# Norm scale and bias taken out of the transitions of a two-layer trunk, and low parts of weights moved to VectorE

## The chip, the cores and the metric

The kernel runs on one core of one Trainium2 chip. TensorE does the matmuls, VectorE, ScalarE and GpSimd the elementwise work, and SyncE (SP in the profile) issues most of the transfers between device memory (HBM) and the core's memory (SBUF); a few are issued by GpSimd. The metric is the time of one execution on the device, in microseconds. The kernel before has a median of 1731.97 us over three runs (1730.14 to 1737.19).

## The reference

One step of a trunk of two layers (`DEPTH` = 2) on 128 context tokens and 512 latent tokens: 640 rows of 1024 numbers, in five tiles of 128 rows (tile 4 holds the context tokens, and comes last in the order of work). Layer 0 mixes tokens by differential attention, layer 1 by neighbourhood attention; each is followed by an MLP with a squared ReLU, 1024 to 4096 and back. Every sub-layer has this form, for latent and context tokens with their own modulation:

```python
h = x * (1 + scale) + shift                                  # scale, shift, gate: SiLU(cond) @ w_mod + b_mod
x = layer_norm(ALPHA * x + gate * sublayer(h), ln_g[i, s], ln_b[i, s])

def layer_norm(x, g, b):
    mu = jnp.mean(xf, -1, keepdims=True)
    var = jnp.mean(jnp.square(xf - mu), -1, keepdims=True)
    return (xf - mu) * lax.rsqrt(var + LN_EPS) * g + b

def sq_relu_mlp(h, w1, w2):
    return jnp.square(jax.nn.relu(h @ w1)) @ w2
```

So there are four norms: after layer 0's attention, after its MLP, after layer 1's attention, and after its MLP (the output). Three of them lie at a transition into a further sub-layer.

## The kernel before

**Precision and weights.** Each operand of a matmul is held as a high part (rounded, `hi`) and a low part (what is left, `lo`), and each product is three matmuls (`mm3`, L119 to L121: high by high, low by high and high by low). Weights come in pieces of 128 x 2 x 512 numbers. `pump` (L175) issues the load of the next piece into one of three buffers `raw` on SyncE; `conv` (L190) has ScalarE cast it to `wh` (L194) and then makes the low part `wl` = raw - `wh` in two halves of 128x512 (L196). `self.pool_lo` says which engine takes a half: with 0 both go to VectorE, with 1 the odd half to GpSimd, with 2 both to GpSimd. A ring of five converted pieces is kept: when the last matmul of a piece is placed, `done` converts the piece that comes five later and issues a further load.

**Order.** TensorE's order is written by hand: `ORDER0`, `ORDER1` and `ORDER_LN` are lists of names, and `run` calls the function that `op` put under each name. What the other engines do is ordered by a scheduler, which sets each instruction into its engine's queue; a queue is worked off in order. So an instruction that waits holds up what stands behind it in its queue.

**Transitions.** X holds the 640 rows in SBUF. In layer 0 and layer 1 the output projection is done in two column halves per tile (o and j in the order lists). `gated` (g) multiplies the product in PSUM by the gate (L1161, into `tmp`), adds it to X (L1163, L1165), takes statistics (L1028), and `ln_pre` makes the mean and variance (L1034), the square root on ScalarE, the reciprocal (L1037), and one pass of 128x1024 over the tile (L1038): (x - mean) * rstd, in place. `norm` (h) calls `ln_h`: TensorE transposes the tile in eight pieces (L1067), ScalarE applies per-row scale and bias while it copies out of PSUM, and the result is split into `hhi` and `hlo` (L127). The norm's own scale g and bias b are at this place folded into the modulation (`mod_affine`), because TensorE needs only h; X itself, which the next residual sum needs, gets them by `affine` in `ln_h`: two passes of 128x1024 per tile on GpSimd (L1078 and L1079). After attention the names of `lnt` hold g and b, the passes of all five tiles are called by the last name of the order list, W (`close`), and the scheduler puts them where they fit. f0 to f3 are the first columns of the MLP's first up chunk.

**MLP (`rest`).** Four groups `gr`; in each, two up chunks of 512 columns (c = 0, 1; `ff`, with `act` for the activation: a Relu on ScalarE, L1224, a product on VectorE, L1225, and a split) and then a down product in two column halves, added to X with the gate (`add_gated_sb`, L1111 to L1117). During attention `pool_lo` is 1, from the swap into the output projection on 2, and in the MLP 1. After the last group of layer 0, `ORDER_LN` runs per tile the second down half (n: `down`), the norm (h: `ln_h`) and the first products of layer 1 (v); here `affine` follows directly and its result goes to device memory (`x1`) for the residual of layer 1.

Of the kernel before, what the change touches and what calls it, by code (L numbers as in the profile page):

```python
# [49 lines left out]
    g1 j02 j13 h0 g2 j03 j04 h1 j14 g3 g4 h2 f0 f2 h3 f3 h4 f1 W  # L50
# [10 lines left out]
    h4 f3 f2 W  # L61
# [4 lines left out]
class Net:  # L66
# [604 lines left out]
    def layer0_attn(self, acc0):  # L671
        nc, a = self.nc, self.a
        with self.tc.tile_pool(name="at0", bufs=1) as pool:
            self.q0 = pool.tile([P, 4, NT], F32R, name="q0")
            self.Vs, self.QKs = {}, {}
            self.pool_lo = 1
# [90 lines left out]
            first4 = self.proj_ops(pool, 0, late, EARLY0, "S73", ("N6", "N7"), ("E0", 2, "E1"), ln)  # L767
# [177 lines left out]
    def layer1_attn(self, pre):  # L945
        nc, a = self.nc, self.a
        with self.tc.tile_pool(name="at1", bufs=1) as pool:
            self.pool_lo = 1
# [24 lines left out]
            def early():  # L973
                self.pool_lo = 2
# [12 lines left out]

            def ln():
                ts = [pool.tile([P, D], F32, tag="PT", name=self.nm("lnt"), bufs=3) for _ in range(2)]
                for t, n in zip(ts, ("lng", "lnb")):  # L990
                    nc.gpsimd.dma_start(t, a[n][1, 0].partition_broadcast(P))
                return ts
# [27 lines left out]
            first4 = self.proj_ops(pool, 1, late, EARLY1, "S73", ("Y", "Z"), ("E", 6, "E"), ln)  # L1020
# [38 lines left out]
    def ln_h(self, pool, X, t, g, b, AB, dst, tag=("hs", 2), now=True):  # L1059
# [57 lines left out]
    def proj_ops(self, pool, l, late, early, free, ready, tag, ln):  # L1117
        nc, n, op = self.nc, NCH * l + 6, self.op
        seq = [(hf, t) for hf in range(2) for t in range(NTT)]
        accs, ms, sb, fs, first, tail = {}, {}, [], [], {}, []  # L1120
# [85 lines left out]
    def rest(self, l, X, first):  # L1206
# [3 lines left out]
        with self.tc.tile_pool(name=f"mlp{l}", bufs=1) as pool:  # L1210
# [9 lines left out]
            def act(us, k, src, cs=None):  # L1220
# [3 lines left out]
                nc.scalar.activation(rv, src, AF.Relu)  # L1224
                nc.vector.scalar_tensor_tensor(rv, src, 0.0, rv, ALU.max, ALU.mult)  # L1225
                self.split(us[0][:, k, cs], us[1][:, k, cs], r[:, cs])
                if not quiet:
                    next(mods, None)

            for gr in range(4):  # L1230
                us = [pool.tile([P, KT, NT], F32R, tag=t, name=self.nm(t)) for t in ("uhi", "ulo")]
                for c in range(2):
                    n = C0 + 8 + 4 * gr + c
                    if gr == 0 and c == 0:
# [9 lines left out]
                        g, b = self.ln_tiles(pool, l, 1)  # L1244
                        st = self.sml.tile([P, NTT, 2, 6], F32, tag="st", name=self.nm("st"), bufs=2)
                        continue
                    for fp in range(2):
                        quiet = gr == 0
                        fs = (2 * fp, 2 * fp + 1)
                        for f in fs:  # L1250
# [12 lines left out]
            def down(t, n):  # L1263
# [150 lines left out]
```

## Time and profile before

| what | value |
|---|---|
| median of three runs | 1731.97 us (1730.14 to 1737.19) |
| profiled execution, its span | 1732.1 us (the page gives no other time of it) |
| TensorE busy | 1645.9 us, 95% |
| VectorE busy | 1131.4 us, 65% |
| ScalarE busy | 662.1 us, 38% |
| GpSimd busy | 594.5 us, 34% |

Busy time is time in which an instruction of the engine was running. The engines work side by side, so these shares don't add up to the span; what an instruction off TensorE costs is seen only where TensorE waits. The trace names the engine, the line, the tiles written and read, and for an idle time the instruction that ended it. The granted clock is a share of TensorE's full clock of 2.4 GHz; 0.50 is its lower level, 1.2 GHz.

### The profile page before, as it was taken

How to read it: one execution, taken by the hardware profiler on the slowest of the kernel's cores; microseconds unless marked ns; L12 is line 12 of the kernel's file. 1: busy time of each engine (PE TensorE's matmuls, PEld its weight loads, DVE VectorE, ACT ScalarE, POOL GpSimd, SP SyncE). 2: the span in 40 equal slices, each digit the busy share in tenths (PEclk: the TensorE clock that was granted, in tenths of full speed). 3: DMA queues.
4: the chain of work that ended last, by engine and by line, in shares of the span. 5: the costliest groups of instructions: out<-in, count | busy, mean ns of one | idle time of the engine just before them, and what ended most of it. 6: DMA issues, size and time to landing. Idle time of an engine off the chain costs nothing.

```text
span 1732.1 us, 25928 instructions
## 1 busy us (share of the span) xinstructions
PE 1645.9 (95%) x10026; PEld 1455.4 (84%) x10026; DVE 1131.4 (65%) x2015; ACT 662.1 (38%) x1338; POOL 594.5 (34%) x457
## 2 busy tenths in 40 slices
PE   8999999999699999999998999998889999999997
PEld 5788888777698988989887889997779898898996
DVE  4788778765848789798557577868685343242338
ACT  2456545643531322221324565655353132131321
POOL 2111012113722337154247243342383133424322
PEclk9999999989899999999999999999989999999999
DMA  8432334233144445454223222223123131212221
GB/s 328 147 118 84 100 113 148 80 112 108 57 133 151 159 146 172 142 164 144 77 83 118 89 78 79 77 85 133 61 92 106 59 98 50 97 56 91 81 66 61
DMA packets 59086, 187.96 MB, mean 109 GB/s; under 512 B 7396, under 2 KB 14034, under 8 KB 57938
## 3 DMA queue, kind: packets, MB, share of 16 engines
q1 hardware_dynamic: 55890, 174.89, 31.3%
q0 software_dynamic: 3072, 11.40, 1.8%
q8 instruction: 79, 1.29, 0.3%
q14 instruction: 45, 0.37, 0.1%
HBM read 176.25 MB, written 7.40 MB: 106 GB/s over the span
## 4 chain that ended last, share of the span: by engine, by line
PE 75%; DVE 14%; issue 4%; POOL 4%; ACT 3%; DMA 1%; SPq 0%; DVEq 0%; POOLq 0%; ACTq 0%
PE M L119 14%; PE M L121 14%; PE M L120 14%; PE S L121 8%; PE S L119 7%; PE S L120 7%; DVE wl L196 4%; PE S L452 2%; PE S L454 2%; POOL wl L196 2%; DVE hlo L127 1%; PE M L589 1%; PE M L259 1%; DVE X L1038 1%; POOL X L1078 1%
## 5 line engine op out<-in xcount | busy, mean ns | idle before, releaser
L196 POOL TENSOR_TENSOR wl<-rw,wh 128x512 fp32r<-128x512 f32 x209 | 345.3, 1672 | 591.4 <-ACT wh L194 541.0
L194 ACT CAST wh<-rw 128x1024 fp32r<-128x1024 f32 x192 | 196.9, 1050 | 348.3 <-PE M L121 268.5
L121 PE MATMUL S<-hhi,wl 128*128 128x320 f32 (+1 forms) x944 | 293.4, 311 | 6.1 <-DVE wl L196 4.7
L119 PE MATMUL S<-hhi,wh 128*128 128x320 f32 (+1 forms) x944 | 292.7, 310 | 0.0
L120 PE MATMUL S<-hlo,wh 128*128 128x320 f32 (+1 forms) x944 | 291.9, 309 | 0.0
L119 PE MATMUL M<-wh,uhi 128*128 128x512 f32 x640 | 249.6, 390 | 1.0 <-ACT uhi L126 1.0
L121 PE MATMUL M<-wh,ulo 128*128 128x512 f32 x640 | 249.3, 389 | 0.3
L120 PE MATMUL M<-wl,uhi 128*128 128x512 f32 x640 | 249.2, 389 | 0.0
L196 DVE TENSOR_TENSOR wl<-rw,wh 128x512 fp32r<-128x512 f32 x175 | 208.9, 1213 | 52.3 <-ACT wh L194 51.3
L119 PE MATMUL M<-wh,hhi 128*128 128x256 f32 (+1 forms) x640 | 202.4, 316 | 9.3 <-DVE tmp L1161 8.4
L121 PE MATMUL M<-wh,hlo 128*128 128x256 f32 (+1 forms) x640 | 196.4, 307 | 3.8 <-DVE hlo L127 3.8
L120 PE MATMUL M<-wl,hhi 128*128 128x256 f32 (+1 forms) x640 | 196.2, 307 | 1.8 <-DVE wl L196 1.8
L121 PEld LDWEIGHTS S<-hhi,wl 128*128 128x128 f32 x944 | 178.9, 189 | 10.1 <-DVE wl L196 8.3
L119 PEld LDWEIGHTS S<-hhi,wh 128*128 128x128 f32 x944 | 179.3, 190 | 0.2
L120 PEld LDWEIGHTS S<-hlo,wh 128*128 128x128 f32 x944 | 179.1, 190 | 0.2
L293 DVE SCALAR_TENSOR_TENSOR jk<-wm,cb 128x1024 bf16<-128x1024 f32 x96 | 142.5, 1484 | 1.5
L121 PEld LDWEIGHTS M<-wh,ulo 128*128 128x128 f32 x640 | 120.2, 188 | 26.3 <-DVE ulo L127 1.1
L119 PEld LDWEIGHTS M<-wh,uhi 128*128 128x128 f32 x640 | 120.2, 188 | 26.2 <-ACT uhi L126 1.9
L120 PEld LDWEIGHTS M<-wl,uhi 128*128 128x128 f32 x640 | 120.1, 188 | 24.6
L119 PEld LDWEIGHTS M<-wh,hhi 128*128 128x128 f32 x640 | 124.2, 194 | 18.6 <-DVE tmp L1161 8.9
L1225 DVE SCALAR_TENSOR_TENSOR r<-S,r 128x640 f32<-128x640 f32 (+1 forms) x62 | 48.4, 781 | 137.8 <-ACT r L1224 137.7
L121 PEld LDWEIGHTS M<-wh,hlo 128*128 128x128 f32 x640 | 123.8, 193 | 11.7 <-DVE hlo L127 7.0
(280 smaller groups left out, 3026.6 us busy)
## 6 DMA issues: line engine op xcount, KB each, us to landing
rw<-in_w SPq DMA_DIRECT2D x192, 512.0 KB, 4.2
wm<-in_wmodT SPq DMA_DIRECT2D x48, 512.0 KB, 3.6
rw<-in_wmod SPq DMA_DIRECT2D x32, 512.0 KB, 4.5
wm<-in_wmod SPq DMA_DIRECT2D x8, 1024.0 KB, 10.5
gate<-gates POOLq DMA_DIRECT2D x6, 512.0 KB, 5.0
X<-in_xT SPq DMA_DIRECT2D x8, 320.0 KB, 11.1
X<-in_xn SPq DMA_DIRECT2D x5, 512.0 KB, 5.4
x<-X SPq DMA_DIRECT2D x5, 512.0 KB, 2.8
```

The lines of the kernel that those rows point to most:

```text
L119: te.matmul(out, sh, mh, start=start, stop=False)
L120: te.matmul(out, sh, ml, start=False, stop=False)
L121: te.matmul(out, sl, mh, start=False, stop=stop)
L127: nc.vector.tensor_tensor(lo, src, hi, ALU.subtract)
L194: keep(nc.scalar.copy(hi, r))
L196: keep(eng.tensor_tensor(lo[:, k], r[:, k], hi[:, k], ALU.subtract))
L259: self.nc.tensor.matmul(acc[32 * j : 32 * j + 32, :256], self.sc[:, 4 * r + j, :], w[:, j, :], start=r == 0, stop=r == 1, tile_position=(0 ...
L293: op = nc.vector.scalar_tensor_tensor(jk, ws[t], 1.0, cb[:, x, :], ALU.mult, ALU.mult, accum_out=mc[:, t, x : x + 1])
L452: te.matmul(out[x], Q[:, x, q], k(K[:, x]), start=True, stop=False)
L454: te.matmul(out[x], Q[r, lo[x], q], k(K[r, x]), start=False, stop=True)
L589: nc.tensor.transpose(t[:, P * (j - j0) : P * (j - j0) + P], E[:, P * j : P * j + P], self.idf)
L1225: nc.vector.scalar_tensor_tensor(rv, src, 0.0, rv, ALU.max, ALU.mult)
```

## The change

1. `pool_lo` is 0 in both attentions, in their output projections too, and 0 from the last down product of an MLP on. In the MLPs it is still 1, and at the program's start still 2. Of 209 low halves on GpSimd 87 move to VectorE.
2. After attention, `close` and the name W are gone, and so are the tiles `lnt`. The ten passes over X (`affine`) are called in the MLP instead, after the Relu of the first column group of the second up chunk in group 0, and the first pass of each tile gets a dependency on that Relu. The tiles `lng` and `lnb` of the MLP are first loaded with this norm's g and b, and loaded anew behind the passes with those of the MLP's norm.
3. At the end of layer 0's MLP, `ln_mid` takes the place of `ln_pre` and the two passes on GpSimd: two passes of 128x1024 on VectorE, (x - mean) * g and x * rstd + b, and the store of the tile directly behind. `mod_affine` for layer 1's attention is then 1 + scale and shift alone.

```diff
@@ ORDER0, and ORDER1 alike
-    g1 j02 j13 h0 g2 j03 j04 h1 j14 g3 g4 h2 f0 f2 h3 f3 h4 f1 W
+    g1 j02 j13 h0 g2 j03 j04 h1 j14 g3 g4 h2 f0 f2 h3 f3 h4 f1
@@ mod_affine
-        pl, ps = (l, 0) if s == 1 else (l - 1, 1)
-        g = self.lnc[:, pl, ps, 0, :].unsqueeze(2).to_broadcast([P, KT, 2])
-        b = self.lnc[:, pl, ps, 1, :].unsqueeze(2).to_broadcast([P, KT, 2])
+        g = self.lnc[:, l, 0, 0, :].unsqueeze(2).to_broadcast([P, KT, 2])
+        b = self.lnc[:, l, 0, 1, :].unsqueeze(2).to_broadcast([P, KT, 2])
+        if s == 0:
+            nc.vector.tensor_scalar(AB[:, 0], sc, 1.0, None, ALU.add)
+            nc.vector.tensor_copy(AB[:, 1], sh)
+            return
@@ layer0_attn, and layer1_attn alike
-            self.pool_lo = 1
+            self.pool_lo = 0
             def swap():
-                self.pool_lo = 2
-            def ln():
-                t = pool.tile([P, 2, D], F32, tag="aTh", name="lnt")
-                for x, n in enumerate(("lng", "lnb")):
-                    nc.gpsimd.dma_start(t[:, x, :], a[n][0, 0].partition_broadcast(P))
-                return t[:, 0, :], t[:, 1, :]
@@ behind ln_pre
+    def ln_mid(self, st, X, t, g, b, dst):
+        nc, x, sml = self.nc, X[:, t, :], self.sml
...
+        nc.vector.bn_aggr(mv, st[:, t, :, :])
+        nc.scalar.activation(rs, mv[:, 1:2], AF.Sqrt, bias=self.eps)
+        nc.vector.scalar_tensor_tensor(x, x, mv[:, 0:1], g, ALU.subtract, ALU.mult)
+        nc.vector.reciprocal(rs, rs)
+        nc.vector.scalar_tensor_tensor(x, x, rs, b, ALU.mult, ALU.add)
+        nc.sync.dma_start(dst, x)
+
+    def affine(self, X, t, g, b, after):
+        nc, x = self.nc, X[:, t, :]
+        op = nc.gpsimd.tensor_tensor(x, x, g, ALU.mult)
+        self.tc.add_manual_dep(
+            op.ins, after.ins.name,
+            mybir.DependencyInfo(mybir.DependencyClass.Sync, mybir.DependencyReason.DATA), reason="affine",
+        )
+        nc.gpsimd.tensor_tensor(x, x, b, ALU.add)
@@ ln_h
-        def affine():
-            nc.gpsimd.tensor_tensor(x, x, g, ALU.mult)
-            nc.gpsimd.tensor_tensor(x, x, b, ALU.add)
-            if dst is not None:
-                nc.sync.dma_start(dst, x)
-
-        if now:
-            affine()
-        return affine
@@ rest
-                        g, b = self.ln_tiles(pool, l, 1)
+                        g, b = self.ln_tiles(pool, l, 0)
...
-                            act(us, 4 * c + f, s2[:, :, :320])
+                            op = act(us, 4 * c + f, s2[:, :, :320])
+                            if gr == 0 and f == 0:
+                                for t in range(NTT):
+                                    self.affine(X, t, g, b, op)
+                                g, b = self.ln_tiles(pool, l, 1)
...
-                    self.ln_pre(st, X, t)
+                    self.ln_mid(st, X, t, g, b, self.x1[t])
...
+            self.pool_lo = 0
             for t in range(NTT):
                 down(t, 0)
```

What this does to the queues is seen at three places. In the rows below x2 is two instructions in a row, `X_4337` the residual, `wl`, `wh` and `rw` a weight's low part, high part and raw piece, `st`, `mv` and `rstd` the norm's statistics. Since lines were taken out and added, L1078/L1079 of before answer to L1042/L1047 of after, L1038 to L1027 (and in the MLP's norm to L1035/L1037), L1028 to L1017, L1034 to L1023 or L1033, L1161 to L1159, L1111/L1115 to L1110/L1114.

GpSimd's queue at the end of the first transition and on into the first MLP, before:

```order
L1078 TENSOR_TENSOR X_4337<-X_4337,lnt 128x1024
L1079 TENSOR_TENSOR X_4337<-X_4337,lnt 128x1024
L1078 TENSOR_TENSOR X_4337<-X_4337,lnt 128x1024
L1079 TENSOR_TENSOR X_4337<-X_4337,lnt 128x1024
L1078 TENSOR_TENSOR X_4337<-X_4337,lnt 128x1024
L1079 TENSOR_TENSOR X_4337<-X_4337,lnt 128x1024
L1214 DMA cb<-srow 128x1024 x2
L1089 DMA gate_932_5430<-gates 128x1024
L1089 DMA gate_933_5432<-gates 128x1024
L1089 DMA lng_5434<-in_lng 128x1024
L1089 DMA lnb_5436<-in_lnb 128x1024
L196 TENSOR_TENSOR wl_5380<-rw_4862,wh_5379 128x512
```

The same place after:

```order
L196 TENSOR_TENSOR wl_5367<-rw_4862,wh_5366 128x512
L196 TENSOR_TENSOR wl_5380<-rw_5002,wh_5379 128x512
L196 TENSOR_TENSOR wl_5393<-rw_5039,wh_5392 128x512
L196 TENSOR_TENSOR wl_5406<-rw_5371,wh_5405 128x512
L1042 TENSOR_TENSOR X_4337<-X_4337,lng_5421 128x1024 x2
L1047 TENSOR_TENSOR X_4337<-X_4337,lnb_5423 128x1024 x2
L1042 TENSOR_TENSOR X_4337<-X_4337,lng_5421 128x1024 x2
L1047 TENSOR_TENSOR X_4337<-X_4337,lnb_5423 128x1024 x2
L1042 TENSOR_TENSOR X_4337<-X_4337,lng_5421 128x1024
L1047 TENSOR_TENSOR X_4337<-X_4337,lnb_5423 128x1024
L1088 DMA lng_5490<-in_lng 128x1024
L1088 DMA lnb_5492<-in_lnb 128x1024
```

Before, the passes stand ahead of the MLP's loads of gates and norm rows, and the MLP's low halves come behind; after, four odd low halves of the MLP come first, then all ten passes together, then two loads, and the next low halves behind these.

VectorE's queue in the first transition, from the statistics of tile 2 to those of tile 3 (`tmp` the gated product), before:

```order
L1034 BN_AGGR mv_4981<-st_4898 128x2
L1163 TENSOR_TENSOR X_4337<-X_4337,tmp_5044 128x512
L1161 TENSOR_TENSOR tmp_5048<-S_4782,gate_4321 128x512
L1037 RECIPROCAL rstd_4983<-rstd_4983 128x1
L127 TENSOR_TENSOR hlo<-hs_5008,hhi 128x4x128
L1038 TENSOR_SCALAR X_4337<-X_4337,mv_4981,rstd_4983 128x1024
L1028 BN_STATS st_4898<-X_4337 128x6
L1165 SCALAR_TENSOR_TENSOR X_4337<-X_4337,tmp_5048 128x512
L127 TENSOR_TENSOR hlo<-hs_5020,hhi 128x4x128
```

The same place after:

```order
L1023 BN_AGGR mv_4978<-st_4898 128x2
L196 TENSOR_TENSOR wl_4998<-rw_4836,wh_4997 128x512 x2
L1026 RECIPROCAL rstd_4980<-rstd_4980 128x1
L127 TENSOR_TENSOR hlo<-hs_5005,hhi 128x4x128
L1027 TENSOR_SCALAR X_4337<-X_4337,mv_4978,rstd_4980 128x1024
L1161 TENSOR_TENSOR X_4337<-X_4337,tmp_5041 128x512
L1159 TENSOR_TENSOR tmp_5045<-S_4782,gate_4321 128x512
L127 TENSOR_TENSOR hlo<-hs_5017,hhi 128x4x128
L196 TENSOR_TENSOR wl_5035<-rw_4849,wh_5034 128x512 x2
L1017 BN_STATS st_4898<-X_4337 128x6
```

Four low halves, which stood in GpSimd's queue, are now between the norm's steps, two ahead of the reciprocal of tile 2 and two ahead of the next statistics.

VectorE's queue in the second transition, tiles 0 and 1 of the norm behind the first MLP (`lng`, `lnb` the norm's rows), before:

```order
L1028 BN_STATS st_5438<-X_4337 128x6
L1034 BN_AGGR mv_8670<-st_5438 128x2
L1037 RECIPROCAL rstd_8672<-rstd_8672 128x1
L1038 TENSOR_SCALAR X_4337<-X_4337,mv_8670,rstd_8672 128x1024
L1111 TENSOR_TENSOR tmp_8701<-M_8676,gate_932_5430 128x512
L1115 TENSOR_TENSOR X_4337<-X_4337,tmp_8701 128x512
L1028 BN_STATS st_5438<-X_4337 128x6
L1034 BN_AGGR mv_8705<-st_5438 128x2
L127 TENSOR_TENSOR hlo<-hs_8712,hhi 128x4x128
L1037 RECIPROCAL rstd_8707<-rstd_8707 128x1
L1038 TENSOR_SCALAR X_4337<-X_4337,mv_8705,rstd_8707 128x1024
```

The same place after:

```order
L1017 BN_STATS st_5425<-X_4337 128x6
L1033 BN_AGGR mv_8668<-st_5425 128x2
L1035 SCALAR_TENSOR_TENSOR X_4337<-X_4337,mv_8668,lng_5490 128x1024
L1036 RECIPROCAL rstd_8669<-rstd_8669 128x1
L1037 SCALAR_TENSOR_TENSOR X_4337<-X_4337,rstd_8669,lnb_5492 128x1024
L1110 TENSOR_TENSOR tmp_8701<-M_8676,gate_932_5417 128x512
L1114 TENSOR_TENSOR X_4337<-X_4337,tmp_8701 128x512
L1017 BN_STATS st_5425<-X_4337 128x6
L1033 BN_AGGR mv_8705<-st_5425 128x2
L1035 SCALAR_TENSOR_TENSOR X_4337<-X_4337,mv_8705,lng_5490 128x1024
L1036 RECIPROCAL rstd_8706<-rstd_8706 128x1
L127 TENSOR_TENSOR hlo<-hs_8714,hhi 128x4x128
```

One pass over the tile behind the reciprocal has become two, the first of which stands ahead of the reciprocal.

## Rows read from the trace of the kernel before

**Rows 1.** the page: span, and busy time of each engine

```profile
span 1732.1 us, 25928 instructions
...
PE 1645.9 (95%) x10026; PEld 1455.4 (84%) x10026; DVE 1131.4 (65%) x2015; ACT 662.1 (38%) x1338; POOL 594.5 (34%) x457
```

**Rows 2.** busy time by stretch: start and end, length, engines, granted clock, DMA

```profile
415.00:475.00 60.00, 44.88 (x243) 38.72 (x242) 52.28 (x66) 29.14 (x69) 44.48 (x26) 0.89 0.19 60
890.00:945.00 55.00, 48.16 (x273) 42.06 (x273) 45.11 (x51) 27.56 (x64) 38.81 (x25) 0.94 0.38 126
1230.00:1302.00 72.00, 59.78 (x335) 53.48 (x334) 57.19 (x73) 34.31 (x78) 45.65 (x25) 0.91 0.22 74
```

**Rows 3.** TensorE's waits, 415 to 475: in total, times, longest

```profile
PE M L1067 <- DVE X L1038: 13.4, 4, 6.6
```

**Rows 4.** TensorE's waits, 890 to 965

```profile
PE S L120 <- DVE wl L196: 3.5, 1, 3.5
```

**Rows 5.** TensorE's waits, 1225 to 1300

```profile
PE M L119 <- DVE tmp L1161: 8.4, 1, 8.4
```

**Rows 6.** VectorE in order of time: start, length, instruction, idle before

```profile
422.27 1.63 DVE L1163 TENSOR_TENSOR X<-X,tmp 128x512 f32<-128x512 f32 x1
423.82 0.68 DVE L1161 TENSOR_TENSOR tmp<-M,gate 128x512 f32<-128x512 f32 x1
424.43 0.68 DVE L1028 BATCH_NORM_STATS2 st<-X 128x6 f32<-128x512 f32 x1
...
428.78 0.81 DVE L1038 TENSOR_SCALAR X<-X,mv,rstd 128x1024 f32<-128x1024 f32 x1
...
444.47 2.83 DVE L1038 TENSOR_SCALAR X<-X,mv,rstd 128x1024 f32<-128x1024 f32 x1
...
461.57 2.07 DVE L1038 TENSOR_SCALAR X<-X,mv,rstd 128x1024 f32<-128x1024 f32 x1
```

**Rows 7.** GpSimd in order of time, 430 to 475

```profile
430.82 2.40 POOL L1078 TENSOR_TENSOR X<-X,lnt 128x1024 f32<-128x1024 f32 x1 [7.46 <-PE M L1067]
...
473.51 0.53 POOL L1089 DMA_DIRECT2D lng<-in_lng  x1
```

**Rows 8.** TensorE in order of time, 445 to 452; then a stretch

```profile
447.35 1.97 PE L1067 MATMUL M<-idf,X 128*128 128x128 f32 x8 [6.63 <-DVE X L1038]
...
926.50:930.00 3.50, 3.46 (x14) 3.17 (x15) 3.50 (x2) 0.71 (x1) 3.50 (x2) 0.50 0.65 177
```

**Rows 9.** TensorE 910 to 940, then VectorE at 527, in order of time

```profile
934.22 1.09 PE L1067 MATMUL M<-idf,X 128*128 128x128 f32 x8 [0.60 <-DVE X L1038]
...
527.14 1.22 DVE L293 SCALAR_TENSOR_TENSOR jk<-wm,cb 128x1024 bf16<-128x1024 f32 x1
```

**Rows 10.** VectorE, TensorE and ScalarE, 1222 to 1320, in order of time

```profile
1247.77 2.21 DVE L1038 TENSOR_SCALAR X<-X,mv,rstd 128x1024 f32<-128x1024 f32 x1
...
1260.09 0.79 PE L119 MATMUL M<-wh,hhi 128*128 128x512 f32 x1 [8.36 <-DVE tmp L1161]
...
1269.82 3.52 PE L1067 MATMUL M<-idf,X 128*128 128x128 f32 x16 [2.56 <-DVE X L1038]
...
1293.65 0.38 ACT L1224 ACTIVATE r<-S 128x256 f32<-128x256 f32 x1 [9.41 <-POOL X L1079]
```

**Rows 11.** the first MLP in order of time: ScalarE, GpSimd, TensorE

```profile
493.84 0.70 ACT L1224 ACTIVATE r<-S 128x640 f32<-128x640 f32 x1 [2.56 <-PE S L121]
...
513.24 5.22 POOL L196 TENSOR_TENSOR wl<-rw,wh 128x512 fp32r<-128x512 f32 x3 [20.07 <-ACT wh L194]
...
514.70 0.39 PE L119 MATMUL M<-wh,uhi 128*128 128x512 f32 x1
...
517.00 0.39 PE L120 MATMUL M<-wl,uhi 128*128 128x512 f32 x1
```

**Rows 12.** GpSimd by line and shape: busy time, mean of one, idle before

```profile
L1079 POOL TENSOR_TENSOR X<-X,lnt 128x1024 f32<-128x1024 f32 x10 | 27.1, 2707 | 0.5
```

**Rows 13.** TensorE's waits, 40 to 415

```profile
PE M L120 <- DVE wl L196: 1.8, 2, 1.3
```

More of the change, by code (lines that the diff above doesn't have):

```diff
@@ L60 @@
     T71 P70 o12 P71 T72 o11 P72 Z o13 j00 j10 j13 g0 j01 j11 j12 g1 j02 h0 g2 j04 j03 g3 h1 j14 g4 h3 h2 f1 f0
-    h4 f3 f2 W
+    h4 f3 f2
 """
@@ L766, in layer0_attn @@
             op("X", swap, "N0", "N1", "N2", "N3", "N4", "N5", "q", "v", "m", "M")
-            first4 = self.proj_ops(pool, 0, late, EARLY0, "S73", ("N6", "N7"), ("E0", 2, "E1"), ln)
+            first4 = self.proj_ops(pool, 0, late, EARLY0, "S73", ("N6", "N7"), ("E0", 2, "E1"))
             self.run(ORDER0)
@@ L947, in layer1_attn @@
         with self.tc.tile_pool(name="at1", bufs=1) as pool:
-            self.pool_lo = 1
+            self.pool_lo = 0
             self.Vs, self.QKs = {}, {}
@@ L973, in early @@
             def early():
-                self.pool_lo = 2
                 pair(7)
@@ L986, in swap @@
                     fn()
[L988 to L992, printed above, removed]
             op = self.op
@@ L1019, in layer1_attn @@
             op("Z", lambda: self.to_h(7, prs[7]["o"]), "Y", "P7", "C7")
-            first4 = self.proj_ops(pool, 1, late, EARLY1, "S73", ("Y", "Z"), ("E", 6, "E"), ln)
+            first4 = self.proj_ops(pool, 1, late, EARLY1, "S73", ("Y", "Z"), ("E", 6, "E"))
             self.run(ORDER1)
@@ L1038, in ln_pre @@
         nc.vector.tensor_scalar(x, x, mv[:, 0:1], rs, ALU.subtract, ALU.mult)
+    def ln_mid(self, st, X, t, g, b, dst):
+        nc, x, sml = self.nc, X[:, t, :], self.sml
+        mv = sml.tile([P, 2], F32, name=self.nm("mv"), tag="mv", bufs=2)
+        rs = sml.tile([P, 1], F32, name=self.nm("rstd"), tag="rstd", bufs=2)
+        nc.vector.bn_aggr(mv, st[:, t, :, :])
[12 more added lines that the diff above has]
+        nc.gpsimd.tensor_tensor(x, x, b, ALU.add)
     def ln_out(self, st, X, t, g, b, dst):
@@ L1057, in ln_out, with ln_h @@
             nc.sync.dma_start(dst[:, c], x[:, c])
-    def ln_h(self, pool, X, t, g, b, AB, dst, tag=("hs", 2), now=True):
+    def ln_h(self, pool, X, t, AB, tag=("hs", 2)):
         nc, h, x = self.nc, self.h, X[:, t, :]
@@ L1115, in add_gated_sb, with proj_ops @@
             eng.tensor_tensor(X[:, t, cs], X[:, t, cs], tmp, ALU.add)
-    def proj_ops(self, pool, l, late, early, free, ready, tag, ln):
+    def proj_ops(self, pool, l, late, early, free, ready, tag):
         nc, n, op = self.nc, NCH * l + 6, self.op
         seq = [(hf, t) for hf in range(2) for t in range(NTT)]
-        accs, ms, sb, fs, first, tail = {}, {}, [], [], {}, []
+        accs, ms, sb, fs, first = {}, {}, [], [], {}
         box = {}
@@ L1153, in gated @@
                 box["st"] = self.sml.tile([P, NTT, 2, 6], F32, tag="st", name=self.nm("st"), bufs=2)
-                box["gb"] = ln()
             X, st = late["X"], box["st"]
@@ L1169, in norm @@
         def norm(t):
-            tail.append(self.ln_h(pool, late["X"], t, *box["gb"], self.AB[l][1], None, (tag[2], tag[1]), False))
+            self.ln_h(pool, late["X"], t, self.AB[l][1], (tag[2], tag[1]))
         def up(f):
@@ L1181, in up @@
             self.ff(NCH * l + 8, f, 0, CUT, fs[f])
-        def close():
-            for fn in tail:
-                fn()
         for x, (hf, t) in enumerate(seq):
@@ L1195, in proj_ops @@
             op(f"f{f}", lambda f=f: up(f), "h0", "h1", "o", "j")
-        op("W", close, "h", "f")
         return fs
@@ L1223, in act @@
                 cs = cs or slice(0, NT)
-                nc.scalar.activation(rv, src, AF.Relu)
+                op = nc.scalar.activation(rv, src, AF.Relu)
                 nc.vector.scalar_tensor_tensor(rv, src, 0.0, rv, ALU.max, ALU.mult)
@@ L1228, in act @@
                     next(mods, None)
+                return op
             for gr in range(4):
@@ L1278, in v @@
                 pre.append(m)
+            self.pool_lo = 0
             for t in range(NTT):
@@ L1288, in rest @@
                 self.op(f"n{t}", lambda t=t: down(t, 1))
-                self.op(f"h{t}", lambda t=t: self.ln_h(pool, X, t, g, b, self.AB[1][0], self.x1[t]), f"n{t}")
+                self.op(f"h{t}", lambda t=t: self.ln_h(pool, X, t, self.AB[1][0]), f"n{t}")
                 if t < 4:
```

## Prediction

> **What bounds the kernel now.** I read the page first: TensorE is busy 1645.9 of 1732.1 us, 95% [rows 1], so only the 86 us in which it stands, and the time below full clock, can be won by work on other engines. The three runs have a median of 1731.97 us; the page gives no time of the profiled execution beside its span, which lies 0.13 us above that median, so the sum is made against 1732.1.
>
> Then busy time by stretch: three transitions hold 34 of the 86 us. From 415 to 475 (layer 0 attention into its MLP) TensorE is busy 44.9 of 60 us at a mean granted clock of 0.89, from 890 to 945 (MLP into layer 1) 48.2 of 55, from 1230 to 1302 (layer 1 attention into its MLP) 59.8 of 72. In all three VectorE is nearly full (52, 45, 57 us) and GpSimd works beside it (44, 39, 46 us) [rows 2]. Last the waits: in the first transition TensorE waits 13.4 us for the normalization L1038, in the second 3.5 us for weight low parts, in the third 8.4 us for a product of VectorE that frees its PSUM bank [rows 3 to 5].
>
> Why VectorE is late there is seen in order of time. Passes of 512 follow one another every 0.61 us when GpSimd rests (423.82 to 424.43), and L1038 takes 0.81; while GpSimd works, an addition takes 1.63 and L1038 2.83 and 2.07 [rows 6]. GpSimd's own pass of 1024 takes 2.40 [rows 7]: VectorE's instruction waits until GpSimd's is done. So GpSimd's 30 passes of scale and bias, for which TensorE hardly waits directly, cost VectorE its speed just where TensorE waits for it.
>
> **First transition.** GpSimd's ten passes leave, and the low parts go to VectorE. Ahead of the last head's scaling stand six halves now, at 0.61 each; the last needs a cast and ends some 1.5 us after the scaling began before, but the step behind it was itself slowed by GpSimd, so TensorE gets the head's last part about 0.7 us late. From there VectorE's own list counts. Up to the L1038 of tile 2 stand 24 passes of 512 (two of them new low halves) x 0.60 = 14.4, three L1038 at 0.81 less an overlap of 0.1, 2.2, and small ones, 0.6: 17.2 us. From 422.2 that ends at 439.4, where before it ended at 444.47 + 2.83 = 447.3. Up to tile 4's: 16 passes, two L1038, small ones and one wait for a square root, 11.9 us, to 451.3, where before it was 461.57 + 2.07 = 463.6 [rows 6]. What TensorE has to do between the two fits in between. Gain 12 us. Bounds: 8, if ScalarE's casts, in whose queue the square roots stand, hold VectorE up at each tile; 14, if the granted clock stays up as well.
>
> **Second transition.** Here one pass of 0.81 becomes two with two inputs each. No such pass of 1024 stands here; the nearest, same operation and length with another output, takes 1.22 us [rows 9]. A tile so costs 2.4 instead of 0.8 alone, but before it ran beside GpSimd, and the square root now hides behind the first pass. Per tile VectorE has three passes of 512, two of 1.2, two low parts of h, 5.5 us and small ones; TensorE has 24 matmuls at 0.23 (ten from 514.70 to 517.00 [rows 11]), 5.5, and 1.1 of transposes. So TensorE should no longer wait for tiles 1 to 3. The 3.5 us for low parts [rows 4] go too, six halves at 0.6 directly behind tile 3, and with them the half clock behind that wait: 0.50 from 926.5 to 930 [rows 8]. What is late next is tile 4: its statistics stand in VectorE's queue behind two low halves whose raw weights are still being loaded. TensorE waits some 3 us there where it waits 0.6 now, and gets to tile 4's transposes at about 927 instead of 934.2 [rows 9]; of these 7 us I give 1 back for the clock behind the new wait. Gain 6; bounds 2 (the two passes bind and the load is late) and 8. The store of x leaves SyncE's queue earlier, at no cost.
>
> **Third transition.** From the second L1038 at 1247.77 to the product behind which TensorE goes on at 1260.09 [rows 10] VectorE has nine passes of 512 and one L1038, 6.2 us when GpSimd rests, so TensorE goes on at about 1254, 6 earlier. The transposes of tiles 2 and 3 came at 1269.82 after a further wait of 2.56 [rows 10], of which some 1.4 go with the slow L1038 (2.21 against 0.81): 1262.4. Three new low halves stand ahead of tile 3's L1038, seven more ahead of tile 4's, in the time in which TensorE has those transposes and the first up chunk's matmuls. Gain 7. ScalarE's wait of 9.41 us for GpSimd's last pass [rows 10], which makes the next casts late, goes as well: 1. Together 8; bounds 5 and 10.
>
> **The MLPs, where time is lost.** The ten passes now stand in GpSimd's queue behind the first wide Relu of the second up chunk, which ends at 493.84 + 0.70 = 494.54. Behind them stand two DMA issues (0.53 each [rows 7]) and the odd low halves of the next chunk, whose matmuls start at 514.70; the first that needs such a half is at 517.00 [rows 11]. So 22.5 us are there. The ten passes take 27.1 by the mean of ten [rows 12], 24.0 at 2.40, about the least [rows 7]. With 1.06 for the DMAs and 1.7 for the half (5.22 / 3 [rows 11]) that is 29.9 or 26.8: TensorE stands 7.4 or 4.3 us. I take 6.5, nearer to the mean, for VectorE has some six passes with two SBUF inputs in that time. Waits like this drop the clock: behind one of 6.63 us the transposes took 1.97 us instead of 1.09, and behind the one of 3.48 it was 0.50 for 3.5 us and more [rows 8, 9]; I put 2 on it. 8.5 us a layer, 17 for both; bounds 10 (no contention, 0.7 for the clock) and 21.
>
> **Attention.** Some 50 halves go from GpSimd to VectorE. A pair took 1.7 us on two engines that block one another; on VectorE alone it takes 1.2. TensorE waited 1.8 us for them up to 415 [rows 13]. I take a gain of 1, bounds a loss of 6 (softmax work stands in VectorE's queue behind halves that wait for casts) and a gain of 4.
>
> The page "SBUF — State Buffer" of the Trainium skill, section "Who interferes with whom", says that a VectorE instruction with two SBUF inputs and a GpSimd instruction that reads SBUF block each other for the whole instruction. By that rule every burst of three pieces in attention gains about 1.4 us, and the second rival's time follows; by the waits in the trace [rows 13] hardly any of it is on TensorE's path.
>
> **Sum.** -12 - 6 - 8 + 17 - 1 = -10: 1722 us.
>
> **Rivals.**
> 1. The passes fit almost into their cover: 4.3 us and 0.7 for the clock a layer, 10 in all instead of 17: 1715. For it: VectorE does little in that chunk. Against: the mean of [rows 12].
> 2. Blocking was dearer in attention than TensorE's waits show, since softmax work in VectorE's queue was late too: a dozen bursts of three pieces x 1.4 us (5.2 against 6 x 0.61 = 3.7) = 17 instead of 1: 1706. Against it: TensorE stands little there.
> 3. VectorE binds the transitions, since low halves wait in its queue for ScalarE's casts, these for TensorE to free a weight buffer, and TensorE for the norm behind. Half of the 26 us are won, 13, and 17 lost: 1736, no change.
> 4. Slower: that ring closes at every tile. Nothing is won in the transitions, and the MLPs cost their 17: 1749. It decides from the point at which low halves hold the norms up by as much as GpSimd did, about 2 us a tile (2.83 against 0.81 [rows 6]). For it: halves stand directly ahead of norms in all three lists. Against: these pieces' buffers come free a tile earlier.
>
> **Chances.** Forecast 0.43, rivals 0.18, 0.09, 0.18 and 0.12. A measurement of this kernel tells 0.5%, 8.7 us, from no change: faster is below 1723.3, slower above 1740.6. The forecast's own range is 1714 to 1730, a little over half of it below 1723.3: 0.23 faster and 0.20 same. Rivals 1 and 2 are faster, 0.27; rival 3 is same; of rival 4, 0.09 slower and 0.03 same. Faster 0.50, same 0.41, slower 0.09. The range leaves out half of rival 2 and most of rival 4: 1706 to 1740.
>
> **What would show it.** In the new trace: no L1038 (now L1027) much over 1 us; tile 4's transposes some 12, 7 and 7 us earlier in the three transitions; ten passes of 2.4 to 2.8 us on GpSimd in each MLP, and right behind them one wait of TensorE of 4 to 8 us for a GpSimd half, with half clock after it. If that wait is missing, or TensorE's waits in the transitions are still 10 us and more, the forecast is wrong.

## The result and the profile after

The changed kernel takes 1725.23 us in the median of five runs (1719.2 to 1728.46), the kernel before 1731.97. The ratio is 0.9943 with a 95% interval of 0.9926 to 0.9961: 7 to 13 us faster.

The page of the changed kernel, to set beside [rows 1]:

```profile
span 1723.4 us, 25882 instructions
...
PE 1645.7 (95%) x10026; PEld 1456.8 (85%) x10026; DVE 1118.9 (65%) x2105; ACT 662.3 (38%) x1338; POOL 428.6 (25%) x360
```

TensorE is busy as long as before; what went is time in which it stood. VectorE runs 90 instructions more and is busy 12.5 us less.

Both kernels issue the same 10026 matmuls in the same order, so a stage can be cut at the start of the same matmul in both. Five such stages, of the kernel before (start and end, length; busy time and count of TensorE, its weight loads, VectorE, ScalarE, GpSimd; granted clock, DMA share, GB/s; a matmul that reaches over an edge is counted on both sides):

```profile
421.58:516.77 95.19, 81.12 (x488) 76.21 (x486) 67.97 (x84) 41.87 (x87) 48.44 (x29) 0.93 0.27 89
516.77:557.57 40.80, 40.80 (x182) 33.78 (x180) 32.64 (x45) 6.00 (x6) 10.53 (x6) 1.00 0.51 166
898.64:950.68 52.04, 45.20 (x275) 40.55 (x274) 41.51 (x46) 28.23 (x67) 39.75 (x28) 0.93 0.32 108
1216.57:1335.60 119.03, 104.99 (x618) 95.99 (x617) 79.08 (x98) 49.74 (x101) 59.70 (x36) 0.94 0.24 79
1335.60:1351.01 15.41, 15.41 (x69) 12.77 (x68) 6.71 (x10) 1.72 (x2) 3.48 (x2) 1.00 0.39 132
```

The same stages after:

```profile
420.57:504.25 83.68, 78.41 (x488) 74.20 (x486) 57.03 (x87) 41.28 (x87) 32.15 (x19) 0.97 0.25 89
504.25:553.44 49.19, 43.06 (x181) 34.84 (x180) 39.53 (x47) 5.99 (x6) 17.06 (x12) 0.93 0.50 160
895.86:944.36 48.50, 44.25 (x275) 40.84 (x274) 33.05 (x54) 28.40 (x68) 9.21 (x19) 0.93 0.35 126
1207.25:1317.79 110.54, 103.03 (x619) 94.49 (x617) 69.72 (x113) 51.09 (x103) 31.15 (x17) 0.98 0.21 71
1317.79:1342.34 24.55, 18.39 (x70) 14.64 (x68) 13.35 (x11) 1.77 (x2) 10.65 (x8) 0.86 0.39 128
```

In order, the change in length in us: first transition -11.5; first down product of the first MLP +8.4; second transition -3.5; third transition -8.5; first down product of the second MLP +9.1.

What VectorE gained is best seen by form. Before, 424 to 476 us (form, count, busy time, mean ns of one):

```profile
L127 DVE TENSOR_TENSOR hlo<-hs,hhi 128x512 fp32r<-128x512 f32 x10 | 13.7, 1374 | 2.3 <-ACT hhi L126 2.3
L1038 DVE TENSOR_SCALAR X<-X,mv,rstd 128x1024 f32<-128x1024 f32 x5 | 10.1, 2020 | 0.0
L1028 DVE BATCH_NORM_STATS2 st<-X 128x6 f32<-128x512 f32 x10 | 6.8, 679 | 0.0
L1165 DVE SCALAR_TENSOR_TENSOR X<-X,tmp 128x512 f32<-128x512 f32 x6 | 4.8, 802 | 0.0
L1163 DVE TENSOR_TENSOR X<-X,tmp 128x512 f32<-128x512 f32 x3 | 4.8, 1586 | 0.0
L1161 DVE TENSOR_TENSOR tmp<-M,gate 128x512 f32<-128x512 f32 x5 | 3.4, 676 | 0.0
```

After, the same stretch:

```profile
L127 DVE TENSOR_TENSOR hlo<-hs,hhi 128x512 fp32r<-128x512 f32 x10 | 6.9, 686 | 4.1 <-ACT hhi L126 4.1
L1017 DVE BATCH_NORM_STATS2 st<-X 128x6 f32<-128x512 f32 x9 | 6.1, 683 | 0.0
L1163 DVE SCALAR_TENSOR_TENSOR X<-X,tmp 128x512 f32<-128x512 f32 x6 | 4.1, 679 | 0.0
L1027 DVE TENSOR_SCALAR X<-X,mv,rstd 128x1024 f32<-128x1024 f32 x5 | 4.0, 804 | 0.0
L1159 DVE TENSOR_TENSOR tmp<-M,gate 128x512 f32<-128x512 f32 x4 | 2.7, 683 | 0.0
L1161 DVE TENSOR_TENSOR X<-X,tmp 128x512 f32<-128x512 f32 x3 | 2.0, 678 | 0.0
```

The split L127 and the addition L1163 (two inputs in SBUF), and the pass over the tile, took two to two and a half times as long beside GpSimd; statistics (one SBUF input) and the gated product (one input in PSUM) took the same in both. The other addition with two SBUF inputs, L1165 (L1163 after), took 0.80 against 0.68: four of its six ran in gaps of GpSimd's queue, at 0.67 to 0.69, the two others took 1.15 and 0.96. The Trainium skill, page "SBUF — State Buffer", section "Who interferes with whom", draws just this line: VectorE blocks against GpSimd with two SBUF inputs, or in the fast modes that its tensor-scalar instruction can enter, and not with one SBUF input. The rows agree form by form.

The price is seen in the first MLP of the changed kernel (`uhi` and `ulo` are the high and low part of the MLP's activation). GpSimd:

```profile
482.10 5.36 POOL L1042 TENSOR_TENSOR X<-X,lng 128x1024 f32<-128x1024 f32 x2 [1.46 <-ACT r L1217]
...
505.68 2.67 POOL L1047 TENSOR_TENSOR X<-X,lnb 128x1024 f32<-128x1024 f32 x1
...
509.42 3.73 POOL L196 TENSOR_TENSOR wl<-rw,wh 128x512 fp32r<-128x512 f32 x3
```

and TensorE:

```profile
504.25 0.39 PE L119 MATMUL M<-wh,uhi 128*128 128x512 f32 x1
510.75 0.80 PE L120 MATMUL M<-wl,uhi 128*128 128x512 f32 x1 [6.11 <-POOL wl L196]
511.34 0.63 PE L121 MATMUL M<-wh,ulo 128*128 128x512 f32 x1
```

The ten passes start 0.1 us after the Relu and end at 508.3. Two issues of loads and one low half later TensorE goes on, 6.1 us late, and the next matmuls take 0.63 instead of 0.39, at the lower of its two clock levels (granted clock 0.50 from 510.75 to 514.3).

### The profile page after: what moved, and what is told of

It reads as the page before. It is cut to its first block, busy times and chain, and to the rows that moved or that the text cites. A ratio compares the mean times of both kernels' runs of the same rounds, so it can differ in the third digit from the quotient of the medians.

```text
span 1723.4 us, 25882 instructions
## 1 busy us (share of the span) xinstructions
PE 1645.7 (95%) x10026; PEld 1456.8 (85%) x10026; DVE 1118.9 (65%) x2105; ACT 662.3 (38%) x1338; POOL 428.6 (25%) x360
## 3 DMA queue, kind: packets, MB, share of 16 engines
q8 instruction: 79, 1.29, 0.3%
## 4 chain that ended last, share of the span: by engine, by line
PE 75%; DVE 11%; POOL 5%; issue 4%; ACT 2%; DMA 2%; SPq 0%; DVEq 0%; POOLq 0%; ACTq 0%
PE M L119 15%; PE M L121 15%; PE M L120 15%; PE S L121 7%; PE S L119 7%; PE S L120 7%; DVE wl L196 4%; PE S L455 2%; PE S L457 2%; POOL X L1042 2%; POOL X L1047 1%; POOL wl L196 1%; DMA rw<-in_w 1%; PE M L259 1%; PE M L592 1%
## 5 line engine op out<-in xcount | busy, mean ns | idle before, releaser
L196 POOL TENSOR_TENSOR wl<-rw,wh 128x512 fp32r<-128x512 f32 x122 | 207.0, 1715 | 423.9 <-ACT wh L194 422.2
L196 DVE TENSOR_TENSOR wl<-rw,wh 128x512 fp32r<-128x512 f32 x262 | 243.5, 967 | 58.4 <-ACT wh L194 56.5
L121 PEld LDWEIGHTS M<-wh,ulo 128*128 128x128 f32 x640 | 121.3, 190 | 26.5 <-DVE ulo L127 1.1
## 6 DMA issues: line engine op xcount, KB each, us to landing
X<-in_xT SPq DMA_DIRECT2D x8, 320.0 KB, 12.5
```

What stands on the lines that cost most here:

```text
L121: te.matmul(out, sl, mh, start=False, stop=stop)
L196: keep(eng.tensor_tensor(lo[:, k], r[:, k], hi[:, k], ALU.subtract))
```

## The experiments

One table first. It gives, for each kernel, the change against the kernel before in six stretches of one profile and in its whole, in us, worked out from the starts of the same matmuls in both profiles, cut as above (a minus is faster); then the median of the timed runs. Left out are what stands ahead of the first transition (-4.9 to +0.9, though most of these kernels are alike there, so a whole profile is known to some 3 us only) and the rest of the MLPs (at most 1.5). Each edit shifts the line numbers by a few; the tiles written and read tell which instruction a row is.

| kernel | first transition | MLP 0, first down | second transition | layer 1 attention | third transition | MLP 1, first down | whole profile | median, us |
|---|---|---|---|---|---|---|---|---|
| changed | -11.5 | +8.4 | -3.5 | -3.0 | -8.5 | +9.1 | -8.7 | 1725.2 |
| lo_only | +5.8 | 0.0 | +0.1 | -1.0 | +7.5 | 0.0 | +13.2 | 1746.0 |
| lo_as_before | -10.8 | +9.6 | -4.6 | -3.3 | -8.2 | +8.9 | -8.6 | 1724.6 |
| vec_halves | -11.7 | +5.9 | -3.8 | -3.3 | -8.2 | +5.9 | -13.8 | 1720.6 |
| no_bias | -10.9 | +0.4 | -3.4 | -2.7 | -6.2 | 0.0 | -20.6 | 1706.7 |
| dummy | +4.9 | +9.5 | -4.3 | -1.5 | +6.9 | +9.0 | +22.2 | 1755.1 |
| mid_back | -11.0 | +8.7 | +0.1 | -0.6 | -8.5 | +8.0 | -6.7 | 1727.9 |
| no_dep | +2.4 | +0.4 | -3.5 | -3.5 | +9.6 | 0.0 | +2.9 | 1737.9 |
| split32 | -10.8 | +2.1 | -3.6 | -3.6 | -8.6 | +1.7 | -24.4 | 1710.3 |
| split_hold | -10.9 | +2.1 | -5.9 | -4.3 | -8.1 | +1.7 | -26.5 | 1708.6 |
| split_min | -12.0 | +2.1 | 0.0 | 0.0 | -7.8 | +1.8 | -16.0 | 1716.2 |

**lo_only: the low halves alone.**

```diff
@@ kernel before: layer0_attn, and layer1_attn alike
-            self.pool_lo = 1
+            self.pool_lo = 0
...
-                self.pool_lo = 2
@@ rest
+            self.pool_lo = 0
             for t in range(NTT):
                 down(t, 0)
```

> The kernel before with the low halves alone moved to VectorE (both attentions, output projections, last down group); the norms' passes stay on GpSimd in the transitions. Theory C (the transitions gain because GpSimd's passes, which VectorE waits out, are gone): the slow L1038 of 2 to 2.8 us stay, VectorE has more to do, TensorE still waits 10 us and more for it in the first and third transitions: 1728 to 1738 us. Rival L (the gain is that low halves no longer wait in GpSimd's queue behind passes): the transitions win their 25 us and no MLP stalls: 1705 to 1712 us.

Measured 1745.99, ratio 1.0073 (1.0058 to 1.0088): 8 us beyond theory C's upper end, and against rival L. TensorE's waits in the third transition (in total, times, longest), to set beside [rows 5], then two low halves on VectorE there:

```profile
PE M L119 <- DVE tmp L1159: 9.0, 1, 9.0
PE M L1065 <- ACT hhi L126: 7.0, 1, 7.0
```

```profile
1277.71 4.07 DVE L196 TENSOR_TENSOR wl<-rw,wh 128x512 fp32r<-128x512 f32 x2 [0.31 <-ACT wh L194]
```

With the passes still there, a half moved to VectorE is one more two-input instruction that can fall beside them (these two took 4.07 us), and a second wait stands beside the old one. Theory C's sign is there only in part: of the fifteen passes like L1038 the longest took 2.70, but the median is 0.81.

**lo_as_before: all but the low halves.**

```diff
@@ changed kernel: layer0_attn, and layer1_attn alike
-            self.pool_lo = 0
+            self.pool_lo = 1
...
+                self.pool_lo = 2
@@ rest
-            self.pool_lo = 0
             for t in range(NTT):
                 down(t, 0)
```

> The changed kernel with the low halves distributed as before, so the passes have left the transitions and the low halves have not. Theory C: most of the transitions' 25 us is kept, some 8 lost to halves that still run on GpSimd beside VectorE, the MLP stalls of 6 us stay: 1724 to 1735 us. Rival L: nothing is won in the transitions and the MLPs cost their 18: 1745 to 1752 us.

Measured 1724.62, ratio 0.9949 (0.9931 to 0.9966), the changed kernel's time, in theory C's range but without the loss of 8 that it expected. Rival L is out. Of the change's three parts the first shows no worth once the passes are gone.

**vec_halves and no_bias: what the stall in the MLP is made of.**

```diff
@@ vec_halves: rest, ahead of each column group of the up chunks
+                            self.pool_lo = 0 if gr == 0 and f == 3 else 1
@@ no_bias: affine
-        nc.gpsimd.tensor_tensor(x, x, b, ALU.add)
```

> The changed kernel with the four low halves that stand behind the ten passes in GpSimd's queue (converted in the last column group of the second up chunk, group 0 of each MLP) put on VectorE. Theory Q (TensorE's wait of 6.1 us in each MLP is GpSimd's queue alone): both waits and the half clock behind them go, 2 x 7.5 to 9: 1707 to 1712 us. Rival P (the passes slow VectorE beside them, so TensorE then waits for VectorE's halves there instead): a wait for a VectorE half of 3 to 6 us stands there, 1718 to 1726 us.

> The changed kernel without the second of the two passes of each tile in the MLP, that is, X goes on without the norm's bias b (left out of the computation). Theory Q: five passes of 2.7 end 13 us earlier, the wait of 6.1 us is gone in both MLPs: 1707 to 1711 us. Rival R (the wait is for the raw weight or the cast, not for the passes in front): the waits stay at 4 us and more, 1719 to 1725 us.

Without the second pass (no_bias leaves b out of X) the time is 1706.72, ratio 0.9856 (0.9833 to 0.9878): 18.5 below the changed kernel by the medians, a little under theory Q's range, and rival R is out. In the profile the stage gets 8.0 and 9.1 shorter, the whole stall. With the halves on VectorE it is 1720.61, ratio 0.9927 (0.9907 to 0.9946), in rival P's range. VectorE there, then TensorE's wait in the first MLP:

```profile
502.12 10.10 DVE L196 TENSOR_TENSOR wl<-rw,wh 128x512 fp32r<-128x512 f32 x6
```

```profile
PE M L120 <- DVE wl L196: 3.4, 2, 1.8
```

Six halves take 1.68 each beside the passes instead of 0.6, and TensorE waits for them twice. So the stall comes from the passes' length, by either road: GpSimd's queue, or VectorE waiting them out.

**dummy: GpSimd's passes put back on a tile that nothing else uses.**

```diff
@@ changed kernel: the name W again at the end of ORDER0 and ORDER1, for this; last is a tile's last transpose
+            for last in tail:
+                first = nc.gpsimd.tensor_tensor(z, z, y, ALU.mult)
+                self.tc.add_manual_dep(
+                    first.ins, last.ins.name,
...
+                )
+                nc.gpsimd.tensor_tensor(z, z, y, ALU.add)
```

> The changed kernel with twenty passes of 128x1024 added on GpSimd, ten in the first and ten in the third transition, each pair behind the transposes of its tile as the old passes were, but on a tile that nothing else reads or writes (loaded by two more transfers). Theory C (VectorE waits out GpSimd's instructions whatever their data): L1038's successor takes 2 us and more again, VectorE with its new halves falls behind as in the run with the low halves alone, 10 to 18 us lost in each of the two: 1745 to 1762 us. Rival D (what the old passes cost came through X: their places in X held up VectorE's or TensorE's work on it): nothing comes back, 1722 to 1729 us.

Measured 1755.1, ratio 1.0127 (1.0097 to 1.0157), in the middle of theory C's range; rival D is out. VectorE, 424 to 476 us:

```profile
L127 DVE TENSOR_TENSOR hlo<-hs,hhi 128x512 fp32r<-128x512 f32 x10 | 15.2, 1531 | 1.1 <-ACT hhi L126 1.1
L1027 DVE TENSOR_SCALAR X<-X,mv,rstd 128x1024 f32<-128x1024 f32 x5 | 6.0, 1195 | 0.0
L1017 DVE BATCH_NORM_STATS2 st<-X 128x6 f32<-128x512 f32 x8 | 5.4, 680 | 0.0
L1167 DVE TENSOR_TENSOR tmp<-M,gate 128x512 f32<-128x512 f32 x3 | 2.0, 681 | 0.0
```

Passes on foreign data bring the slow forms back (the pass L1027 1.20 in the mean instead of 0.80, at most 2.28) and leave the others alone. Both transitions lose some 16 us (-11.5 to +4.9, -8.5 to +6.9), and TensorE's two long waits in the third are those of lo_only, 9.0 and 7.0 us.

**mid_back: the norm behind the MLP as before.**

```diff
@@ changed kernel: rest, with mod_affine as in the kernel before
-                    self.ln_mid(st, X, t, g, b, self.x1[t])
+                    self.ln_pre(st, X, t)
@@ behind ln_h of each tile
+                nc.gpsimd.tensor_tensor(x, x, g, ALU.mult)
+                nc.gpsimd.tensor_tensor(x, x, b, ALU.add)
+                nc.sync.dma_start(self.x1[t], x)
```

> The changed kernel with the norm behind layer 0's MLP as before: one VectorE pass, then two GpSimd passes and the store, scale and bias folded into the modulation again; all low halves there still on VectorE. Theory C: the second transition falls back to the time of the kernel before or a little worse, since VectorE waits out ten passes: 4 to 8 us slower than the changed kernel, 1728 to 1734 us. Rival V (the second VectorE pass is itself what limits there, so the old form is better now that GpSimd holds no low halves): 1718 to 1723 us.

Measured 1727.85, ratio 0.9963 (0.9948 to 0.9977), just under theory C's range. By the medians the part is worth 2.6 us, less than two timings tell apart; by the stages it is 3.6 in the transition and 2.4 behind it. Rival V is not borne out.

**no_dep: the passes without their wait.**

```diff
@@ changed kernel: affine
-        op = nc.gpsimd.tensor_tensor(x, x, g, ALU.mult)
-        self.tc.add_manual_dep(
-            op.ins, after.ins.name,
...
-        )
+        nc.gpsimd.tensor_tensor(x, x, g, ALU.mult)
```

> The changed kernel without the dependency of the ten passes on the Relu: they are called at the same place, but each waits only for its data, so they start at about 466 us, some 16 us earlier, two tiles ahead of the first chunk's low halves and the rest between them. Theory Q (only the end of the ten passes in GpSimd's queue counts): the last ends ahead of the halves that TensorE needs, both waits of 6.1 us go: 1707 to 1713 us. Rival W (early passes stand ahead of halves for the second up chunk and beside VectorE's activation work, so a new wait takes the place): a wait of 3 to 8 us for a GpSimd half or for ulo or uhi between 470 and 500, 1718 to 1728 us.

Measured 1737.86, ratio 1.0024 (1.0013 to 1.0035): slower than the kernel before, rival W and worse than it said. The old waits are gone (+0.4, 0.0) and dearer ones stand earlier. TensorE's waits, 425 to 530, then 1290 to 1335 us:

```profile
PE S L121 <- POOL wl L196: 11.7, 3, 7.7
```

```profile
PE S L121 <- POOL wl L196: 15.8, 1, 15.8
```

In the second MLP all ten passes, from 1280.1 to 1305.8, stand in the queue ahead of the next halves. So the dependency on the Relu is no cost in itself: it keeps four halves in front.

**split32: three tiles' passes, then halves, then two tiles' passes.**

```diff
@@ changed kernel: rest
-                            if gr == 0 and f == 0:
-                                for t in range(NTT):
+                            if gr == 0 and f in (0, 3):
+                                for t in range(3) if f == 0 else range(3, NTT):
                                     self.affine(X, t, g, b, op)
-                                g, b = self.ln_tiles(pool, l, 1)
+                                if f == 3:
+                                    g, b = self.ln_tiles(pool, l, 1)
```

> The changed kernel with the passes of tiles 0 to 2 behind the first Relu as now, and those of tiles 3 and 4 behind the fourth Relu of the chunk; in GpSimd's queue three of the four odd halves that TensorE waited for then stand between them. Theory Q: the six passes end at 498, the halves follow at once, and the wait is gone: 1708 to 1713 us. Rival P (VectorE's own halves, slowed by passes beside them, are late in any case): 2 to 4 us of wait per MLP remain, 1715 to 1720 us.

Measured 1710.27, ratio 0.9859 (0.9844 to 0.9874), as theory Q said. GpSimd, then TensorE's waits, in the first MLP:

```profile
493.87 2.42 POOL L1047 TENSOR_TENSOR X<-X,lnb 128x1024 f32<-128x1024 f32 x1
499.33 5.22 POOL L196 TENSOR_TENSOR wl<-rw,wh 128x512 fp32r<-128x512 f32 x3 [3.04 <-ACT wh L194]
504.50 5.31 POOL L1042 TENSOR_TENSOR X<-X,lng 128x1024 f32<-128x1024 f32 x2
```

```profile
PE M L121 <- DVE ulo L127: 1.4, 1, 1.4
PE S L121 <- DVE wl L196: 0.5, 1, 0.5
```

Three halves now wait for their casts alone. The fourth comes behind the last passes, at 515.4, and TensorE doesn't wait for it.

**split_hold: tile 4's norm ahead of the low halves.** On top of split32, the four pieces that the last down product of layer 0 uses up are converted after the norm of tile 4 is placed:

```diff
@@ used
-            self.done(g)
+            if self.hold is None:
+                self.done(g)
+            else:
+                self.hold.append(g)
@@ down, first line, then behind ln_mid
+                self.hold = [] if n and t == 4 and not l else None
+                held, self.hold = self.hold or [], None
+                for w in held:
+                    self.done(w)
```

> The kernel with the passes split three and two, and besides, at the end of layer 0's MLP the four pieces of weights that the last tile's product uses up are converted after that tile's norm is placed: in VectorE's queue the product of tile 4, its statistics and its two passes come ahead of or between the low halves instead of behind seven of them. Theory H (TensorE's wait of 4.3 us for tile 4 in the second transition, and the half clock behind it, is VectorE's queue): the transposes come 2 to 4 us earlier: 1704 to 1708 us. Rival N (the halves are then late for layer 1's next products, and TensorE waits for them instead): 1709 to 1713 us, with a wait for a VectorE half between 925 and 945.

Measured 1708.55, ratio 0.9849 (0.9826 to 0.9872). Its interval overlaps that of split32, so by time this is open; the profile shows both at work. TensorE's wait for tile 4 in the second transition was 4.1 us in split32; now the only one between 895 and 945 is

```profile
PE S L121 <- DVE wl L197: 2.3, 3, 1.2
```

(L197 is L196 one line on.) Theory H's wait is gone. A wait for VectorE's halves, of rival N's kind, has come instead (from 910 to 914 in this profile), at about half that length, and the stage is 2.3 us shorter.

**split_min: one part alone, split.**

```diff
@@ kernel before: ORDER0, and ORDER1 alike
-    g1 j02 j13 h0 g2 j03 j04 h1 j14 g3 g4 h2 f0 f2 h3 f3 h4 f1 W
+    g1 j02 j13 h0 g2 j03 j04 h1 j14 g3 g4 h2 f0 f2 h3 f3 h4 f1
@@ rest, with affine as in the changed kernel
+                            if gr == 0 and f in (0, 3):
+                                for t in range(3) if f == 0 else range(3, NTT):
+                                    self.affine(X, t, g, b, op)
```

> The kernel before with one part of the change alone: the ten passes behind each attention leave the transitions, and go into the MLP split three and two. Low halves stand where they stood before, and so does the norm behind layer 0's MLP with its GpSimd passes. Theory C with the parts added up (split three and two 1710.3, low halves back 0, norm in the middle back 2.6): 1711 to 1717 us. Rival I (the parts need one another: GpSimd's halves beside the old middle norm cost what they did before, and halves on GpSimd beside the norms cost 2 us a tile): 1718 to 1726 us.

Measured 1716.16, ratio 0.9901 (0.9885 to 0.9917), at the upper end of theory C's range. Its gains are where they were (-12.0 and -7.8), and the second transition and layer 1's attention stay as in the kernel before.

## Why the prediction was right

**What bounds the transitions** held, and is shown: VectorE slowed by GpSimd's passes while TensorE waits for it. Ten passes per transition on idle data bring the slowdown back (dummy), with the passes gone and the halves where they were the gain stays (lo_as_before, split_min), and in the changed kernel no L1027 takes over 0.82 us.

**First transition**: 12 forecast, 11.5 measured; tile 4's transposes come at 452.38 against 463.69. Before, then after:

```profile
463.69 1.31 PE L1067 MATMUL M<-idf,X 128*128 128x128 f32 x8 [3.39 <-DVE X L1038]
```

```profile
452.38 1.04 PE L1076 MATMUL M<-idf,X 128*128 128x128 f32 x8
```

The two marks that the prediction set for VectorE, 439.4 and 451.3, were met at 438.9 and 451.3 (three passes of 0.81 less 0.1 are 2.3 and not 2.2, which changes neither):

```profile
438.12 0.81 DVE L1027 TENSOR_SCALAR X<-X,mv,rstd 128x1024 f32<-128x1024 f32 x1
...
450.49 0.81 DVE L1027 TENSOR_SCALAR X<-X,mv,rstd 128x1024 f32<-128x1024 f32 x1
```

The new halves between the norm's steps cost TensorE nothing that shows there (-10.8 without them, in lo_as_before).

**Second transition**: 6 forecast, 3.5 in the stage. The wait for tile 4, forecast at some 3, is

```profile
PE M L1076 <- DVE X L1037: 4.3, 1, 4.3
```

and its transposes come 8.6 earlier than in [rows 9], of which 2.8 stood already: 5.8, not 7.

```profile
925.58 1.94 PE L1076 MATMUL M<-idf,X 128*128 128x128 f32 x8 [4.25 <-DVE X L1037]
...
927.20:930.50 3.30, 3.30 (x17) 3.30 (x16) 0.69 (x1) 3.27 (x9) 0.00 (x0) 0.50 0.39 129
```

The clock behind the new wait, priced at 1, was mis-sized too: transposes of 1.94 instead of 1.09 and, in the second row, a granted clock of 0.50, together some 2. What the step did not see: about 2.4 us more come back behind the transition. Before, GpSimd's work for layer 1 started late, and TensorE waited 1.6, 1.3 and 0.9 us for low halves and a cast between 950 and 1030; after, it doesn't. With the old norm back nearly all of the gain of 3.0 in layer 1's attention is gone (mid_back -0.6, split_min 0.0), and with the halves back it stays (lo_as_before -3.3), so it belongs to the norm. By which waits is shown only in part: in split_min they stand again, but in mid_back only 0.5 us of them do, and 2.4 us are lost all the same. So the part was worth about 6 after all, by luck, for 2.4 of it lie outside the stage that the 6 were forecast for.

**Third transition**: 8 forecast, 8.5 measured; TensorE's wait of 8.4 [rows 5] is

```profile
PE M L119 <- DVE tmp L1159: 3.2, 1, 3.2
```

**The MLPs**: 17 forecast, 8.4 + 9.1 = 17.5 in the profile; no_bias gives 8.0 + 9.1 of it back. The wait came where it was put and as long (6.1 and 6.2, against 6.5). Rival 1, the passes almost inside their cover, is out: they took 26.2 us (482.1 to 508.3), near the mean of [rows 12] and not near the 24.0 that it took from [rows 7]. What the prediction didn't forecast is how cheaply the loss is avoided: three tiles before the halves and two after give 14 of it back (6.3 and 7.4).

**Attention**: a gain of 1 forecast for the moved halves. The run without that part (lo_as_before) takes 0.6 us less, so nothing shows, and rival 2 (17 us hidden in attention) is out with it. In the transitions the prediction priced the halves with the passes, as one change; it had no term for halves moved while the passes stay, which is the part's real danger (lo_only, some 13 us).

**Rivals 3 and 4**, the ring of halves, casts and norms, are out for the changed kernel, whose transitions gain 23.5 of the 26 that were forecast. Times like theirs come only where passes run beside the moved halves, in lo_only and dummy; that it is the ring that costs there isn't shown.

The sum, -10, stands against -8.7 in the profile and -7 to -13 in the timed runs. That it comes so near is in part luck: 2.5 too much for the second transition and 1.8 too little for the MLPs' loss (0.5 in the stages, 1.3 late in the first MLP) stand against 3 more than forecast in the two attentions (-1.0 and -3.0 for a forecast of 1). By the prediction's own mark, 1723.3, the time falls on the side of no change (chance 0.41) and not of faster (0.50), though the interval of the ratio leaves out 1. Open is 1.3 us lost late in the first MLP, behind a wait of 3.5 us that both kernels have. Before, the granted clock is 0.54 in the 3 us behind that wait and 1.00 in the next 3; after, it is 0.50 and 0.57. The same loss, 1.3 to 1.5, stands in no_bias, mid_back, no_dep and the three split runs, and not in lo_only and dummy (0.2 and 0.3); why isn't known.

## What to carry to other kernels

An engine that TensorE hardly ever waits for can still set TensorE's pace, by slowing the engine that TensorE does wait for: look for one form with two durations, and for what ran beside the longer one. Work moved out of a tight stretch must be laid out in its new queue by what stands behind it: put pieces that others wait for first, and cut the rest so that it fits the gaps. And take a change of several parts apart before keeping it: here one part earned nothing that shows, and alone it cost some 13 us.

## What the runs showed of the hardware

Moving work from GpSimd to VectorE was no relief while GpSimd had other long instructions: a low half took 1.68 us on VectorE beside the passes (six in 10.10, in vec_halves), as long as on GpSimd itself, 1.715 in the mean of 122 in the changed kernel:

```profile
L196 POOL TENSOR_TENSOR wl<-rw,wh 128x512 fp32r<-128x512 f32 x122 | 207.0, 1715 | 423.9 <-ACT wh L194 422.2
```

On VectorE with GpSimd idle it is 0.6 (two in 1.29 at 920.88 of the changed kernel). Three that fell beside the passes in the changed kernel, from 500.67 on, took 2.70 to 2.85 us each (8.22 together), as long as a pass of GpSimd.
